# Two hybrid decoder layers on one core: the next mixer's first products on unnormalised h in both halves, six weight blocks split ahead and kept in DRAM, and another order of GpSimd memsets

## The chip, the core and the metric

The kernel runs on one core of a Trainium2 chip. The core has a matrix engine (TensorE, PE in the profile; its weight loads are PEld), VectorE (DVE), ScalarE (ACT), GpSimd (POOL) and a queue engine (SyncE, SP) that here issues nearly all DMAs. Each engine works through its own queue in order, and engines wait for one another by semaphores. The metric is the device time of one execution in microseconds; lower is better.

## What is computed

The reference is two layers of a trunk with 528 tokens (16 learned meta tokens and 512 real ones) and width 1024. Cut to what matters here:

```python
def rms_norm(x, g):
    return x * rsqrt(mean(x * x, -1) + 1e-6) * g

def mixer_sublayer(h, pre_g, post_g, w_in, ...):
    u = rms_norm(h, pre_g)
    z = u @ w_in
    q, k, v, f_logit, a_val, a_gate, sc_b, sc_c, sc_x = split(z)
    y_attn = forgetting_attention(q, k, v, log_sigmoid(f_logit + b_forget))
    a = a_val * sigmoid(a_gate)
    y_conv = silu(layer_norm(causal_depthwise_conv(a, 31 taps))) @ a_pw_w
    y_sc = sc_b * causal_depthwise_conv(sc_c * sc_x, 3 taps)
    y = head_rms_norm(concat[y_attn, y_conv, y_sc]) @ w_out
    return h + rms_norm(y, post_g)

def ffn_sublayer(h, pre_g, post_g, w_up, conv_w, w_down):
    z = causal_depthwise_conv(rms_norm(h, pre_g) @ w_up, 3 taps)
    g, up = split(z)
    return h + rms_norm((silu(g) * up) @ w_down, post_g)

for l in range(2):
    h = mixer_sublayer(h, ...); h = ffn_sublayer(h, ...)
```

The factor of a norm is one number per token. So w_in can be applied to h times the gain before the factor is known, and the product multiplied by the factor afterwards; a gate or a convolution needs the factor before its own non-linear step.

## The kernel before

Everything lies transposed: 128 partitions hold channels, the free axis holds the 528 tokens. h is a tile of eight k-blocks of 128 channels. Tokens are worked on in two halves of 264. Each float32 operand is split into a high part (a copy rounded to the matmul's format) and the rest, hi and lo, and each product is three matmuls, hi·hi, hi·lo and lo·hi, in `mm3` (L656). Weights come from DRAM in blocks of 128 output columns, 128 x 1024 for a full one: SP loads `raw` (3 buffers), ACT casts it to `whi`, DVE subtracts to `wlo`. The tiles `whi`/`wlo` come from a pool of three (`wp`) or, for some blocks, from a second pool of five on the other side of the memory (`wide_pool`, `wx`). Within the plain FFN loops this is `prep_one` (L506 to L509), two blocks ahead; elsewhere it is `plan_block` (L618 to L626).

The order of the engines' queues is written at build time by a planner, `Flow`. Work for ACT, DVE, POOL and SP is entered with an estimated duration, what it waits for, and a priority (a smaller number goes first); matmuls come from generators ("threads"), of which the earliest listed one that is ready goes on. The planner follows time with its estimates and fixes one order per engine. What it doesn't know, such as the reuse of memory by a later tile or the order of GpSimd's memsets, is waited for on the chip.

The place of the change is the step from layer 0's FFN to layer 1's mixer.

- `finish` (L1728) computes the last third of the FFN's down projection. `products` issues, for output blocks 0 and 1, both halves, then blocks 2 to 7 for half 0, then blocks 2 to 7 for half 1. `evac` (L1692) adds each result to `yp`, squares it on ACT (L744) and scales it by the post gain (L1695).
- `post_norm` forms the norm factor of y for a half. `Norms.factor` sums the squares by a matmul with a constant matrix (L793) and then needs three steps on ACT (L803, L806, L807) and two on DVE (L808, L814). Then yp is multiplied by it (L870) and added to h (L880), by pairs of k-blocks. h is squared again for the next norm, and goes to DRAM (`h_dram`) for a later use.
- `gained` (L823) writes h times layer 1's gain into yp, two ACT steps for each pair. `pre_norm` forms h's factor, multiplies yp by it on DVE (L835), casts to `uhi` on ACT (L837) and subtracts to `ulo` on DVE (L838).
- `first_half` issues layer 1's first six products for half 0: a_gate 0, a_val 0, a_gate 1, a_val 1, then sc_c 0 and sc_x 0. `First.steps` takes blocks 0 and 1 together, then blocks 2 to 5 together, going through k with all blocks of the group.
- `mixer` takes half 1 of the same six blocks (`firsts`): 0 and 1, then 2 and 3 when the gate of half 0 that holds their banks is done, then 4 and 5. `Front.gated` (L925 to L939) turns gate and value into the input `apad` of the 31-tap convolution: exp, log and exp on ACT, and a product on DVE. It can also take the norm factor, and does so for layer 0's half 0, where the factor is multiplied in twice on DVE. The 31 taps on two tiles (L969, L972) are low in priority on DVE. `sc_c` and `sc_x` evacuate blocks 4 and 5.
- After that, the pool `ap` of the attention opens, POOL clears its tiles (L418 and L1191 among them), and `fill` works through v, q, k and the rest by `mixer_steps`. v's first product also gives the forget gate's logits: DVE adds the bias into `fx` (L1217), and a chain from there (L1248 to L1262) has two small matmuls (L1261 the second).

Memory around it: `fp` holds the FFN's tiles, yp, rz (the factor), four tiles z, h, squares. The next mixer's tiles take the place of fp's; ap's take that of the five wide weight slots.

Of the kernel before, what the change touches and what calls it, by code (L numbers as in the profile page):

```python
# [9 lines left out]
F32 = mybir.dt.float32  # L10
# [5 lines left out]
P = 128  # L16
# [56 lines left out]
def chunk_list():  # L73
# [3 lines left out]
    for l in range(DEPTH):  # L77
# [5 lines left out]
        for kind, j in mixer_steps():  # L83
# [45 lines left out]
def mixer_steps():  # L129


    return [("sc_c", 0), ("sc_x", 0), ("v", 0), ("q", 0), ("k", 0), ("sc_b", 0), ("q", 1),
            ("k", 1), ("q", 2), ("k", 2), ("v", 1), ("q", 3), ("pw", 0), ("k", 3), ("sc_c", 1), ("sc_x", 1), ("sc_b", 1)]
# [56 lines left out]
class When:  # L190
# [170 lines left out]
def tile_hybrid_trunk(ctx: ExitStack, tc: tile.TileContext, xT, wflat, pv_d, out):  # L361
# [149 lines left out]

    def prefetch(n):
# [71 lines left out]
    coming = deque()  # L584

# [23 lines left out]
    def plan_block(i, prio):  # L609
# [18 lines left out]

        got = flow.op("sp", dma_us(sz), load, prio=prio, lat=dma_lat(sz), takes=[(raws, slot)])
        ring = split["pw"][chunks[i][1]] if chunks[i][0] == "a_pw_w" else split["wide" if i in wide else "rot"]  # L630
# [3 lines left out]
        a = act(act_us(sz), high, got, *after, prio=prio, takes=[(ring, b.slot)])  # L634
# [33 lines left out]
    class First:  # L668
# [9 lines left out]
        def alone(self, hf, both, *ids):  # L678
# [3 lines left out]
            for j, i in enumerate(ids):  # L682
                self.ps[hf, i] = t[:, j, :self.n[hf]] if both else t[:, :self.n[hf]]
                yield [self.ws[i].tok]
                for k in range(KD):
                    yield [When(lambda: self.at.get((hf, k)))]
# [139 lines left out]
    def pre_norm(norms, key, hg, hg_at, a, z, at, hf, prio):  # L826

        n = z - a
        yield from norms.factor(key, n)
        s = norms.sums[key]  # L830

        def pair(k, prio):
            y = hg[:, k:k + 2, a:z]
            hi = uhi[:, k:k + 2, a:z]
            f = dve(dve_us(2 * n), lambda: nc.vector.tensor_mul(y, y, s["r"].unsqueeze(1).to_broadcast([P, 2, n])),  # L835
                    s["r_at"], *hg_at[hf, k], prio=prio)
            c = act(act_us(2 * n), lambda: nc.scalar.copy(hi, y), f, prio=prio)  # L837
            d = dve(dve_us(2 * n), lambda: nc.vector.tensor_sub(ulo[:, k:k + 2, a:z], y, hi.bitcast(F32)), c, prio=prio)  # L838
            at[hf, k] = [c, d]
            return f  # L840

        s["free"].close(*[pair(k, prio + 0.01 * k) for k in range(0, KD, 2)])

    def post_norm(norms, key, nkey, h, h_at, a, z, yp, g, g_next, at, hf, prio, out_at, y_out, on_pe=()):
# [99 lines left out]
    def mixer(l, ypool, first, close_first, spans, front=None, rz0=None):  # L944
# [1143 lines left out]
```

## Time and profile before

| | |
|---|---|
| median of 3 runs | 1301.95 us (1300.68 to 1302.2) |
| the profiled execution | 1301.88 us, span 1300.2 us |
| mean granted TensorE clock | 0.997 |
| busy: PE, DVE, ACT, POOL | 1278.3, 852.7, 612.2, 96.2 us |
| weight loads by SP | 160 of 512 KB, 32 of 448 KB, 4 of 528 KB, 2 of 256 KB |

A row of a timeline has start, duration (of all instructions that it merges), engine, line, operation, output<-input, shapes, count, and in brackets the idle time before it with what ended it. A row of the waits has who waited for whom, the total in us, how often, and the longest. A row of windows has, for each engine, busy time and in brackets the count of instructions. Matmuls overlap in the records: the time between two starts is what one costs, not its duration.

The layers stand in the span like this: layer 0's mixer to about 222 us, its FFN to about 651 us, layer 1's mixer to about 870 us, then layer 1's FFN. The down projections of FFN parts 0 and 1 of layer 0 begin near 360 and 488 us.

### The profile page before, as it was taken

How to read it: one execution, taken by the hardware profiler on the slowest of the kernel's cores; microseconds unless marked ns; L12 is line 12 of the kernel's file. 1: busy time of each engine (PE TensorE's matmuls, PEld its weight loads, DVE VectorE, ACT ScalarE, POOL GpSimd, SP SyncE). 2: the span in 40 equal slices, each digit the busy share in tenths (PEclk: the TensorE clock that was granted, in tenths of full speed). 3: DMA queues.
4: the chain of work that ended last, by engine and by line, in shares of the span. 5: the costliest groups of instructions: out<-in, count | busy, mean ns of one | idle time of the engine just before them, and what ended most of it. 6: DMA issues, size and time to landing. Idle time of an engine off the chain costs nothing. (4 is left out here: it accounts for less than half of the span.)

```text
span 1300.2 us, 23941 instructions
## 1 busy us (share of the span) xinstructions
PE 1278.3 (98%) x9802; PEld 1226.7 (94%) x9802; DVE 852.7 (66%) x1449; ACT 612.2 (47%) x1143; POOL 96.2 (7%) x254
## 2 busy tenths in 40 slices
PE   8999999999999999999989999999999999999997
PEld 8999899999999999999989998899999799989997
DVE  7798765687624663566676877757786256636664
ACT  7254577654423432344662645866543234314443
POOL 1313311000000000000003133100000000000000
PEclk9999999999999999999989999999999999999999
DMA  6136132502232222223340361334032332232321
GB/s 238 34 100 158 50 99 78 201 18 98 82 98 83 96 79 101 95 83 100 105 142 18 108 166 43 97 125 147 18 103 92 97 88 89 72 122 86 92 72 65
DMA packets 46637, 124.75 MB, mean 96 GB/s; under 512 B 5616, under 2 KB 15984, under 8 KB 46528
## 3 DMA queue, kind: packets, MB, share of 16 engines
q1 hardware_dynamic: 46480, 123.10, 30.7%
q8 instruction: 77, 1.26, 0.4%
q14 instruction: 32, 0.26, 0.1%
q0 software_dynamic: 48, 0.13, 0.0%
HBM read 108.04 MB, written 4.33 MB: 86 GB/s over the span
## 5 line engine op out<-in xcount | busy, mean ns | idle before, releaser
L656 PE MATMUL psum<-uhi,whi 128*128 128x264 f32 (+1 forms) x1936 | 454.9, 287 | 2.8 <-ACT uhi L837 1.1
L656 PE MATMUL psum<-ulo,whi 128*128 128x264 f32 (+1 forms) x1936 | 449.2, 285 | 0.8 <-DVE ulo L1869 0.4
L656 PE MATMUL psum<-uhi,wlo 128*128 128x264 f32 (+1 forms) x1936 | 447.3, 284 | 0.0
L656 PEld LDWEIGHTS psum<-uhi,whi 128*128 128x128 f32 x1936 | 324.0, 189 | 8.2 <-issue 1.9
L656 PEld LDWEIGHTS psum<-ulo,whi 128*128 128x128 f32 x1936 | 325.0, 189 | 1.9 <-DVE ulo L1869 0.6
L656 PEld LDWEIGHTS psum<-uhi,wlo 128*128 128x128 f32 x1936 | 324.8, 189 | 0.0
L656 PE MATMUL psum<-yhi,whi 128*128 128x264 f32 (+3 forms) x888 | 247.7, 302 | 1.4 <-ACT yp L2020 1.0
L656 PE MATMUL psum<-yhi,wlo 128*128 128x264 f32 (+3 forms) x888 | 245.4, 299 | 0.7 <-DVE wlo L626 0.7
L656 PE MATMUL psum<-ylo,whi 128*128 128x264 f32 (+3 forms) x888 | 245.0, 298 | 0.0
L508 ACT CAST whi<-raw 128x1024 fp32r<-128x1024 f32 (+1 forms) x110 | 113.3, 1031 | 214.7 <-PE psum L656 200.3
L509 DVE TENSOR_TENSOR wlo<-raw,whi 128x1024 fp32r<-128x1024 f32 (+1 forms) x110 | 132.0, 1200 | 81.7 <-ACT whi L508 79.7
L656 PEld LDWEIGHTS psum<-yhi,whi 128*128 128x128 f32 x888 | 159.0, 188 | 8.7 <-ACT yp L2020 1.4
L656 PEld LDWEIGHTS psum<-yhi,wlo 128*128 128x128 f32 x888 | 159.1, 188 | 6.4 <-DVE wlo L626 1.1
L656 PEld LDWEIGHTS psum<-ylo,whi 128*128 128x128 f32 x888 | 159.3, 188 | 5.4
L1969 DVE SCALAR_TENSOR_TENSOR c<-z,pv,c 128x528 f32<-128x528 f32 (+1 forms) x176 | 131.9, 756 | 2.7
L626 DVE TENSOR_TENSOR wlo<-raw,whi 128x1024 fp32r<-128x1024 f32 (+2 forms) x86 | 102.5, 1204 | 33.6 <-ACT whi L622 30.9
L622 ACT CAST whi<-raw 128x1024 fp32r<-128x1024 f32 (+2 forms) x86 | 87.9, 1030 | 31.1 <-PE psum L656 19.7
L972 DVE SCALAR_TENSOR_TENSOR cacc<-apad,pv,cacc 128x528 f32<-128x528 f32 x120 | 87.6, 771 | 0.2
L1987 ACT CAST yhi<-c 128x528 fp32r<-128x528 f32 (+1 forms) x44 | 27.6, 627 | 108.6 <-DVE c L1983 108.6
L1979 ACT ACTIVATE c<-c 128x528 f32<-128x528 f32 (+1 forms) x44 | 28.1, 639 | 79.3 <-DVE c L1969 79.3
L1967 ACT ACTIVATE c<-z,pv 128x528 f32<-128x528 f32 (+1 forms) x88 | 63.3, 726 | 0.4 <-DVE z L1935 0.4
L1932 DVE TENSOR_TENSOR z<-psum,rz 128x528 f32<-128x528 f32 x40 | 28.3, 708 | 53.7 <-PE psum L656 52.2
(214 smaller groups left out, 1417.2 us busy)
## 6 DMA issues: line engine op xcount, KB each, us to landing
raw<-in_w_dram SPq DMA_DIRECT2D x160, 512.0 KB, 3.6
raw<-in_w_dram SPq DMA_DIRECT2D x32, 448.0 KB, 3.5
h<-in_x_dram SPq DMA_DIRECT2D x16, 264.0 KB
q<-pair_hi SPq DMA_DIRECT2D x24, 132.0 KB, 2.2
k<-pair_hi SPq DMA_DIRECT2D x24, 132.0 KB, 2.4
raw<-in_w_dram SPq DMA_DIRECT2D x4, 528.0 KB, 3.4
h_dram<-h SPq DMA_DIRECT2D x4, 528.0 KB
h<-h_dram SPq DMA_DIRECT2D x8, 264.0 KB, 5.8
```

Of the source, the lines that this page charges most:

```text
L508: nc.scalar.copy(hi[:, :sz], raw[:, :sz])
L509: nc.vector.tensor_sub(lo[:, :sz], raw[:, :sz], hi[:, :sz].bitcast(F32))
L622: nc.scalar.copy(box["hi"][:, :sz], box["raw"][:, :sz])
L626: nc.vector.tensor_sub(lo[:, :sz], box["raw"][:, :sz], box["hi"][:, :sz].bitcast(F32))
L656: nc.tensor.matmul(d, lhsT=w[a][:, k, cols], rhs=rhs(b, k, hf), start=start and i == 0 and p == 0, stop=stop and i == n - 1 and p == 2)
L972: nc.vector.scalar_tensor_tensor(conv[j], in0=src, in1=conv[j], scalar=col("a_dw_w", CK * j + i), op0=ALU.mult, op1=ALU.add)
L1932: nc.vector.tensor_mul(two(t[:, off:]), srcs[0], two(rz))
L1967: nc.scalar.activation(dst, src[:, 2:2 + 2 * fw], AF.Copy, scale=wtap(2, t))
L1969: nc.vector.scalar_tensor_tensor(dst, in0=src[:, i:i + 2 * fw], scalar=wtap(i, t), in1=dst, op0=ALU.mult, op1=ALU.add)
L1979: silu = nc.scalar.activation(cs[0], cs[0], AF.Silu)
L1987: nc.scalar.copy(ghi, cs[0])
```

## The change

**First products.** In the step between the layers, `post_norm` now writes h times the next gain, unnormalised, split into hi and lo, for both halves (`to=raw[hf]`): two scaled copies on ACT and two scalar_tensor_tensor on DVE for each pair, right behind L880. The tiles are the seven of the FFN's gated product, the down projection's right-hand side, and one more. `First` reads them. h's factor goes into `rz` for both halves and the normalised uhi and ulo follow with priorities 2.4 to 2.6, where they had 0 to 1.1. In the mixer the gates of both halves, and `sc_c`, get the factor (`rzs`): two DVE multiplications more for each gate, and two in place of an ACT copy for `sc_c`. yp and rz move to a pool `hg` on the wide slots' side, which closes with them; the second scratch of the norms is z0. `first_half` takes blocks 2 and 3, then 4, then 5 one after the other. The mixer's run goes on until u is planned.

**Weights.** `MASK` picks layer 1's first six w_in blocks. In layer 0's FFN, after every second output block of the down projections of parts 0 and 1, `store_one` splits one that was fetched the time before, writes hi and lo to DRAM from GpSimd's queue, and fetches the next raw block. Later `plan_block` loads hi and lo of these six straight into their weight tiles by two DMAs on SP, with no cast or subtraction.

**Memsets.** fx, gt and p4 of the mixer are made and cleared directly after vals, ahead of causal, k, q and dm, in both layers.

`mixer_steps` now looks up one list per layer; both lists are the old one.

```diff
+MASK = "111111000000000000000000"
...
+class Ahead:
+    def __init__(self, tok, by):
+        self.tok, self.by = tok, by
+    @property
+    def time(self):
+        return None if self.tok.time is None else self.tok.time - self.by
...
+    to_store = deque(i for i, c in enumerate(chunks) if c[1] == 1 and c[0] == "w_in" and MASK[sum(d[:2] == c[:2] for d in chunks[:i])] == "1")
+    stored = {}
+    fetched = deque()
+    def store_one():
+        if fetched:
+            i, sz, raw = fetched.popleft()
+            hi, lo = (T(wx[0], [P, WCHUNK], F32R, t) if sz <= WCHUNK else T(wp, [P, CHUNK], F32R, t) for t in ("whi", "wlo"))
+            nc.scalar.copy(hi[:, :sz], raw[:, :sz])
+            nc.vector.tensor_sub(lo[:, :sz], raw[:, :sz], hi[:, :sz].bitcast(F32))
+            stored[i] = T(dram, [P, 2, sz], F32, f"w_split{i}")
+            for n, t in enumerate((hi, lo)):
+                nc.gpsimd.dma_start(stored[i][:, n], t[:, :sz].bitcast(F32))
+        if to_store:
+            i = to_store.popleft()
+            sz = chunks[i][3] * chunk_cols(chunks[i])
+            raw = T(wp, [P, CHUNK], F32, "raw", 3)
+            nc.sync.dma_start(raw[:, :sz], wflat[offs[i]:offs[i] + P * sz].rearrange("(p s) -> p s", p=P))
+            fetched.append((i, sz, raw))
...
+        if i in stored:
+            def fetch(n):
+                if n == 0:
+                    box["w"] = [wtile(i, t) for t in ("whi", "wlo")]
+                    b.w = tuple(t[:, :sz].rearrange("p (k n) -> p k n", n=n_cols) for t in box["w"])
+                nc.sync.dma_start(box["w"][n][:, :sz].bitcast(F32), stored[i][:, n])
+            n_cols, lat = n, dma_lat(sz)
+            got = flow.op("sp", dma_us(sz), lambda: fetch(0), taken.get(id(ring), ()), prio=prio, lat=lat, takes=[(ring, b.slot)])
+            taken[id(ring)] = issued = [Ahead(got, lat)]
+            b.tok = flow.op("sp", dma_us(sz), lambda: fetch(1), issued, prio=prio, lat=lat)
+            coming.append((i, b))
+            return
...
@@ post_norm
-                    hi, lo, gc = uhi[:, k + i, a:z], ulo[:, k + i, a:z], g_next[:, k + i:k + i + 1]
+                    hi, lo = (uhi[:, k + i, a:z], ulo[:, k + i, a:z]) if to is None else (to[0][k + i], to[1][k + i])
+                    gc = g_next[:, k + i:k + i + 1]
...
@@ mixer
-                gated(1, j, first.tok[1, 2 * j + 1])
+                gated(1, j, first.tok[1, 2 * j + 1], rzs[1], zero)
...
-                gated(0, j, first.tok[0, 2 * j + 1])
+                gated(0, j, first.tok[0, 2 * j + 1], rzs[0], zero)
...
-                evacs += use(hf, first.ps[hf, i], first.tok[hf, 5], rz0 if hf == 0 else None)
-        flow.run(lambda: all(t.time is not None for t in evacs + list(gated_at.values())))
+                evacs += use(hf, first.ps[hf, i], first.tok[hf, 5], rzs[hf])
+        flow.run(lambda: all(t.time is not None for t in sum(u_at.values(), evacs + list(gated_at.values()))))
...
         mset(vals[:, :, :, DH:], 1.0)
+        fx = T(ap, [P, 5, HEADS], F32, "fx")
+        nc.gpsimd.memset(fx, 0.0)
+        gt = T(ap, [P, 5, HEADS], F32, "gt")
+        p4 = [T(ap, [P, N_META], F32, f"p4{i}") for i in range(2)]
+        for t in p4:
+            mset(t, 0.0)
...
@@ finish
-                hg_at = {(hf, k): gained(h, yp, a, z, k, gpre, out_at[hf, k], hf + 0.05 + 0.01 * k) for k in range(0, KD, 2)}
-                yield from pre_norm(norms, ("h", hf), yp, hg_at, a, z, first.at, hf, hf)
+                late = rzs[hf] is not None
+                hg_at = {(hf, k): gained(h, yp, a, z, k, gpre, out_at[hf, k], (2.4 if late else 0.05) + hf * (0.1 if late else 1) + 0.01 * k)
+                         for k in range(0, KD, 2)}
+                yield from pre_norm(norms, hf, n[hf], yp, hg_at, rzs[hf], u_at if late else first.at, 2.5 + 0.1 * hf if late else hf)
...
@@ first_half
-            yield from first.steps(0, (True, 2, 3), (False, 4), (False, 5))
+            yield from first.alone(0, True, 2, 3)
+            for i in (4, 5):
+                yield from first.alone(0, False, i)
...
-            yp = T(fp, [P, KD, L], F32, "yp", 1)
+            hp = wxs.enter_context(tc.tile_pool(name=f"hg{l}", bufs=1, side="right", reuse_waits="tile"))
+            rz, yp = T(hp, [P, L], F32, "rz"), T(hp, [P, KD, L], F32, "yp")
...
+                        if l == 0 and m%2:
+                            store_one()
...
+                    if not final:
+                        raw = [[g[f0 + k][b] for k in range(nf)] + [T(ypool, [P, L], F32R, f"y{n}{nf}")] for b, n in enumerate(("hi", "lo"))]
+                        raw = [[[t[:, half_sl(hf)] for t in ts] for ts in raw] if hf < 2 else None for hf in range(2)]
+                        rzs = [rz[:, half_sl(hf)] if raw[hf] else None for hf in range(2)]
+                        first = First(lambda b, k, hf, raw=raw: raw[hf][b][k] if raw[hf] else u_rhs(b, k, hf), [H, H], {})
...
-                        norms.factors([rs, rz], h=APART)
+                        norms.factors([rs, zs[0][:, 2:]], h=APART)
```

More of the change, by code (lines that the diff above doesn't have):

```diff
@@ L633, in plan_block @@
             after, prio = [coming[-1][1].tok], URGENT
-        a = act(act_us(sz), high, got, *after, prio=prio, takes=[(ring, b.slot)])
+        a = act(act_us(sz), high, got, *after, *(taken.get(id(ring), ()) if stored else ()), prio=prio, takes=[(ring, b.slot)])
+        taken[id(ring)] = [a]
         b.tok = dve(dve_us(sz), low, a, prio=prio)
@@ L1189, in mixer @@
             dms.append(dm)
-        fx = T(ap, [P, 5, HEADS], F32, "fx")
-        nc.gpsimd.memset(fx, 0.0)
-        gt = T(ap, [P, 5, HEADS], F32, "gt")
         g_hl = [T(mp, [P, L], F32, "sq", 2)[:HEADS].bitcast(F32R) for _ in range(2)]
-        p4 = [T(ap, [P, N_META], F32, f"p4{i}") for i in range(2)]
-        for t in p4:
-            mset(t, 0.0)
         v_at = {}
@@ L1776, in ends @@
             yield from post_norm(norms, ("y", hf), None if first is None else ("h", hf), h, [] if merge else list(h_at.values()), a, z, yp,
-                                 gpost if merge and not GA else None, None if merge else gpre, first and first.at, hf, hf, out_at, y_out, (0, 2) if alone and hf else ())
+                                 gpost if merge and not GA else None, None if raw and raw[hf] is None else gpre, first and first.at,
+                                 hf, hf, out_at, y_out, (0, 2) if alone and hf else (), raw and raw[hf])
             if first is None:
```

58 lines of the change are left out of this document (30 added, 28 removed), and 3 rows, old and new, of the table ORDERS.

## Prediction

> **What bounds the kernel now.** I read the page first, then the stages by windows, then TensorE's timeline where its share drops, then the two engines that feed it.
>
> ```profile
> span 1300.2 us, 23941 instructions
> PE 1278.3 (98%) x9802; PEld 1226.7 (94%) x9802; DVE 852.7 (66%) x1449; ACT 612.2 (47%) x1143; POOL 96.2 (7%) x254
> ```
>
> TensorE sets the end: 98% busy, with 21.9 us idle in all. A change that leaves the products alone can only win from those 21.9 us and from stretches at a reduced clock. The stage of the change is 605 to 720 us; columns below are busy time and count of PE, PEld, DVE, ACT, POOL, then granted clock, DMA share, GB/s.
>
> ```profile
> 640.00:650.00 10.00, 10.00 (x74) 9.61 (x73) 9.71 (x14) 8.81 (x18) 0.00 (x0) 1.00 0.41 128
> 650.00:660.00 10.00, 6.53 (x31) 5.28 (x30) 8.54 (x16) 9.24 (x19) 0.00 (x0) 0.71 0.41 141
> 660.00:670.00 10.00, 10.00 (x79) 10.00 (x79) 9.63 (x13) 6.89 (x14) 0.00 (x0) 0.95 0.67 220
> 670.00:680.00 10.00, 10.00 (x75) 9.61 (x74) 5.25 (x9) 3.30 (x7) 0.00 (x0) 1.00 0.31 101
> 680.00:690.00 10.00, 10.00 (x85) 10.00 (x84) 4.49 (x8) 5.01 (x11) 0.18 (x2) 1.00 0.17 55
> 710.00:720.00 10.00, 9.20 (x77) 8.83 (x76) 9.78 (x23) 5.32 (x11) 0.00 (x0) 1.00 0.29 75
> ```
>
> One row stands out: 31 matmuls in 650 to 660, where neighbours have 74 and 79, and a granted clock of 0.71. TensorE's timeline there:
>
> ```profile
> 648.39 1.05 PE L793 MATMUL psum<-c,om_d 128*128 128x264 f32 x4
> 649.09 0.48 PE L656 MATMUL psum<-yhi,whi 128*128 128x264 f32 x1
> 649.41 0.29 PE L656 MATMUL psum<-ylo,whi 128*128 128x264 f32 x1
> ...
> 650.87 0.28 PE L656 MATMUL psum<-ylo,whi 128*128 128x264 f32 x1
> 650.99 0.28 PE L656 MATMUL psum<-yhi,wlo 128*128 128x264 f32 x1
> 653.49 1.42 PE L793 MATMUL psum<-acc,om_d 128*128 128x264 f32 x4 [2.22 <-DVE acc L753]
> 656.01 0.59 PE L656 MATMUL psum<-uhi,whi 128*128 128x264 f32 x1 [1.09 <-ACT uhi L837]
> 656.75 0.59 PE L656 MATMUL psum<-ulo,whi 128*128 128x264 f32 x1 [0.15 <-DVE ulo L838]
> ...
> 660.88 0.38 PE L656 MATMUL psum<-ulo,whi 128*128 128x264 f32 x1
> 661.09 0.29 PE L656 MATMUL psum<-uhi,wlo 128*128 128x264 f32 x1
> ```
>
> The last product of layer 0's FFN issues at 650.99, the first of layer 1 at 656.01, because the normalised input of half 0 is not there. Then the matmuls are slow until 661.09: 20 of them from 656.01 on, where the spacing before the gap was 0.12 us (650.87 to 650.99).
>
> What half 0 waits for is a chain on ACT and DVE:
>
> ```profile
> 639.42 0.70 DVE L880 TENSOR_TENSOR h<-h,yp 128x528 f32<-128x528 f32 x1
> 645.98 0.70 DVE L880 TENSOR_TENSOR h<-h,yp 128x528 f32<-128x528 f32 x1
> 646.60 3.49 DVE L626 TENSOR_TENSOR wlo<-raw,whi 128x1024 fp32r<-128x1024 f32 x3
> 652.39 0.43 DVE L814 SCALAR_TENSOR_TENSOR rz<-rz 128x264 f32<-128x264 f32 x1
> 655.99 1.55 DVE L838 TENSOR_TENSOR ulo<-yp,uhi 128x528 fp32r<-128x528 f32 x2
> ```
>
> The new h of half 0 is there pair by pair from 640.1 to 646.7 (L880), but its norm factor only at 652.8 (L814), and scaling and splitting (L835, L837, L838) follow.
>
> **Part 1, first products on unnormalised h.** The factor leaves the path. Now each pair of k needs, behind L880, two scaled copies on ACT and two subtractions on DVE; the factor multiplies the products later, in the evacuations. Nearest rows for these two and for the next steps of half 1:
>
> ```profile
> L823 ACT ACTIVATE yp<-h,pg x16: 500/502/505, 640.7 to 669.6; 128x264 f32<-128x264 f32 x16
> 658.41 0.42 DVE L814 SCALAR_TENSOR_TENSOR rs<-rs 128x264 f32<-128x264 f32 x1
> 659.38 2.35 DVE L626 TENSOR_TENSOR wlo<-raw,whi 128x1024 fp32r<-128x1024 f32 x2
> 661.65 1.32 DVE L870 TENSOR_TENSOR yp<-yp,rs 128x528 f32<-128x528 f32 x2
> 680.73 0.71 DVE L838 TENSOR_TENSOR ulo<-yp,uhi 128x528 fp32r<-128x528 f32 x1 [0.70 <-ACT uhi L837]
> 683.65 0.42 DVE L939 TENSOR_TENSOR apad<-psum,cxp 128x264 f32<-128x264 f32 x1
> ```
>
> Half 0: 8 copies of 0.50 (4.0 us ACT) and 8 subtractions of 0.42 (3.4 us DVE) between 640 and 650. DVE drops the 3.49 us of weight splits at 646.60 there (part 2), so it breaks even; the last pair should be split at about 649.5 (645.98 + 0.70 + 3.4 at the most 650.1), and the product loop reaches it only after three earlier pairs. I take no wait at 651. TensorE then runs: 650.99 + 0.12, the four norm matmuls of half 1's y (648.39 to 649.41 holds four of them and one product, so 1.02 - 0.12 = 0.90 us), and 20 matmuls of 0.122: the twenty-first at 651.11 + 0.90 + 2.44 = 654.45 instead of 661.09. **Gain 6.6 us**: the gap and the half clock together.
>
> Half 0's six blocks are 144 matmuls, 17.5 us, and the twelve norm matmuls of h (0.225 each, 2.7 us) fall among them: TensorE wants half 1 at 651.1 + 0.9 + 17.5 + 2.7 = 672.2. Half 1's y factor is done at 658.8 (L814) at the latest; then 4 multiplications, 4 additions (0.66 each by L870's 1.32 for two) and 8 subtractions of 0.42 are 8.6 us of DVE: 667.4, without the 2.35 us of splits that stood ahead of them. Cover 4.8 us. If it were gone, every microsecond shows.
>
> Behind that, the gates (L925 to L939) of half 0 must clear banks before blocks 2 and 3 of half 1 can start, at 672.2 + 5.9 = 678.1. Today they sit behind ulo (680.73) and end at 684.07. They get two DVE multiplications by the factor each (0.42 x 4 = 1.7 us): their present 683.65 + 0.42 - 681.44 = 2.6 us become some 4.3 us from 672.2, 676.5. Cover 1.6 us, thin. The eight gates' multiplications and four of sc_c (replacing two ACT copies) add 12 x 0.42 = 5.0 us of DVE.
>
> Normalised u is still made, for v, q and k, now last in priority: over both halves 16 copies on ACT, 8 multiplications, 8 casts and 8 subtractions, as before. v starts at 672.2 + 17.5 = 689.7. DVE has 9.7 us of work in 670 to 690 today, so 10 us are free for what is left of it. I cost it at nothing; what hides it are half 1's 17.5 us of products.
>
> **Part 2, six blocks split in the FFN.** Six loads on SP's queue, six casts on ACT and six subtractions on DVE move to the down projections of FFN parts 0 and 1; twelve stores of 512 KB are new on POOL's queue; between the layers twelve loads of 512 KB on SP replace six.
>
> ```profile
> 389.47 1.05 ACT L508 CAST whi<-raw 128x1024 fp32r<-128x1024 f32 x1 [4.31 <-PE psum L656]
> 390.55 1.22 DVE L509 TENSOR_TENSOR wlo<-raw,whi 128x1024 fp32r<-128x1024 f32 x1 [4.63 <-ACT whi L508]
> 395.33 1.05 ACT L508 CAST whi<-raw 128x1024 fp32r<-128x1024 f32 x1 [4.32 <-PE psum L656]
> raw<-in_w_dram SPq DMA_DIRECT2D x160, 512.0 KB, 3.6
> ```
>
> In the FFN a block lasts 395.33 - 389.47 = 5.86 us and ACT and DVE idle 4.3 and 4.6 of them; 1.05 and 1.22 more at every second block fit. A raw buffer is held between two such steps, so the stream runs on two of three for that long: a load may then start when the block two earlier is split, 5.9 us (1.05 + 1.22 + 3.6) before it lands, and it has two blocks, 11.7 us. POOL does nothing in the FFN; the stores have 100 us before they are read. Cost 0; bounds 0 and six exposed splits, 6 x 2.27 = 13.6 us.
>
> Between the layers the loads wait for a weight slot, freed by the last product on it, and SP's queue behind them holds h's stores and v's loads. The last slot frees at 651.1; two loads, estimated at twice 3.6 us, land by 658.3, and block 5 is wanted at 652.0 + 14.6 = 666.6. Nothing.
>
> **Part 3, memset order.**
>
> ```profile
> DVE fx L1217 <- POOL p L418: 12.2, 2, 6.3
> 692.46 1.04 POOL L418 MEMSET vals<- 128x528 f32 x2
> 704.91 0.14 POOL L1191 MEMSET fx<- 128x40 f32 x1
> PE psum L1261 <- DVE fpre L1256: 1.7, 2, 0.9
> ```
>
> In both mixers DVE's queue stands for about 6 us behind fx, whose clearing needs 0.14 us but comes on POOL's queue 12.4 us after vals, behind the memsets for k, q and dm. Clearing it right after vals, near 693.5 in today's times, takes away that stall. DVE has slack at its end, so most of the 12.2 us are worth nothing; what TensorE loses later is the wait for fpre, 1.7 us in two places, when DVE has caught up too late. fx's last addition would come some 2 us earlier, more than 0.9. **Gain 1.7 us**, bounds 0 and 1.7.
>
> **Sum.** 1301.88 (the profiled execution; span 1300.2 and 1.68 around it; the median of the runs, 1301.95, is 0.07 above) - 6.6 - 1.7 = 1293.6. For the thin cover at the gates and for small misses of an order fixed beforehand I add 0.5, between 0 and 3.3 (today's two idle times at this place, 2.22 + 1.09): **1294.1 us**.
>
> **Rivals.** *B: part of the gap stays.* TensorE runs in order; if half 1's norm matmuls are put ahead of the first products, as today, they again wait for acc, 2.22 us, and 1.09 us may follow for the last splits. Against it: half 0's splits are ready by then, so the products can be put first. Price 3.3 us, 1297.4; with the slow matmuls again (20 x 0.10 = 2.0), 1299.4. Here the granted clock fell to half after a 2.22 us gap, four matmuls and a 1.09 us gap, so I count the 2.0. The Trainium skill (TensorE: Matmul & The Clock Gate, Part 1) says the clock halves after an idle window of about 3.4 us; by that, a single gap of 2.2 us would cost only itself, 1296.3, and the trace agrees with it only if its two gaps count as one.
>
> *C: the wait moves to the gates or to half 1.* Cover 1.6 and 4.8 us; a late u op or two ahead of a gate (0.7 each) and scratch shared with the norms speak for it. Taken at 2 us: 1296.1.
>
> *D: slower, through the FFN's weight stream.* If the held buffer keeps a block's split behind TensorE's need, the six steps are exposed: 13.6 us, 1294.1 + 13.6 = 1307.7. It decides once a load needs over 11.7 - 2.3 = 9.4 us to land where the row has 3.6, so I give it little.
>
> *E: hidden anyway.* From 705 us DVE is the busy engine (9.78 of 10 in 710 to 720) and feeds attention. If it, not TensorE, paces that stage, the 6.6 us come back as waits there and only part 3 remains: 1301.9 - 1.7 = 1300.2. For it: 5.0 us more DVE work. Against: its 6.3 us stall behind fx falls away in the same stretch, and TensorE is 92% busy even there.
>
> **Chances.** A, the forecast, 0.55 (its own range 1292.4 to 1295.6); B 0.16; C 0.12; E 0.09; D 0.08. This measurement cannot tell under 0.2%, 2.6 us, from no change: faster is below 1299.3, slower above 1304.6. Faster: A, C and nearly all of B, 0.82. Same: E and B's edge, 0.10. Slower: D, 0.08. The range reaches from 1291.5 (A with 2 us of further relief on DVE in attention) to 1299.4 (B's dear end), leaving out D, E and little below.
>
> **What would show it.** Right: no TensorE idle over 1 us between the last down product and the first with the new input, granted clock 1.00 throughout there; v starting about 6.6 us earlier; fx's wait on POOL and fpre's wait gone in both layers; FFN parts 0 and 1 of layer 0 as long as before. Wrong: a wait for hi, lo or a loaded block at 651 or near 672, for a gate near 678, gaps at the FFN's blocks, or the gain shrinking between v and the output projection.

## The result, and the profile after

The changed kernel takes 1294.19 us (median of 4 runs, 1293.85 to 1294.39); the kernel before, run beside it, 1301.84 us (4 runs, 1300.68 to 1302.2). The ratio is 0.9942, 95% interval 0.993 to 0.9954: faster by 7.65 us. 1294.1 was predicted. The profiled execution has a span of 1292.0 us, 8.2 less than the 1300.2 of before.

The head of the page:

```profile
span 1292.0 us, 24062 instructions
PE 1274.1 (99%) x9802; PEld 1223.7 (95%) x9802; DVE 864.3 (67%) x1477; ACT 618.1 (48%) x1157; POOL 103.1 (8%) x266
```

TensorE does the same 9802 matmuls. Its idle time falls from 21.9 to 17.9 us and its busy time by 4.2 us; slow matmuls at the half clock count as busy (before, 660 to 661 us: 6 matmuls at clock 0.50, busy 1.00). VectorE has 11.6 us more work and ScalarE 5.9 us, and the kernel is faster all the same. The stage of the change, by windows, with the columns of the table before:

```profile
640.00:650.00 10.00, 10.00 (x78) 9.74 (x77) 8.87 (x17) 8.84 (x20) 0.00 (x0) 1.00 0.96 337
650.00:660.00 10.00, 10.00 (x78) 9.74 (x77) 6.99 (x15) 7.91 (x20) 0.00 (x0) 1.00 0.74 282
660.00:670.00 10.00, 10.00 (x75) 9.61 (x74) 8.69 (x16) 7.29 (x17) 0.00 (x0) 1.00 0.31 108
670.00:680.00 10.00, 9.31 (x76) 9.10 (x76) 8.73 (x18) 8.03 (x18) 0.18 (x2) 1.00 0.01 2
```

In 650 to 660 stand 78 matmuls at a granted clock of 1.00, where 31 stood at 0.71. TensorE's timeline at the old gap:

```profile
651.07 0.28 PE L712 MATMUL psum<-ylo,whi 128*128 128x264 f32 x1
651.19 0.28 PE L712 MATMUL psum<-yhi,wlo 128*128 128x264 f32 x1
651.32 1.05 PE L849 MATMUL psum<-acc,om_d 128*128 128x264 f32 x4
652.20 1.05 PE L849 MATMUL psum<-c,om_d 128*128 128x264 f32 x4
652.90 0.48 PE L712 MATMUL psum<-yhi,whi 128*128 128x264 f32 x1
```

The norm matmuls on acc, for which TensorE had waited 2.22 us, now issue without a wait. Both traces have 8520 products in `mm3`; the 4441st, the first of layer 1, stood at 656.01 behind the gap, and is now at 648.24, 0.12 us behind the one before it: eighteen products on the unnormalised pairs (the last two of them above) go ahead of the norm. A new, small wait shows 20 us later, in the row of TensorE's timeline at the start of half 1:

```profile
672.27 0.39 PE L712 MATMUL psum<-yhi,whi 128*128 128x264 f32 x1 [0.69 <-DVE z L864]
```

To see where the time went, the n-th matmul of one trace is set against the n-th of the other: the table gives its start before and the shift after. A step between two rows is time won or lost between these two matmuls. (In 5150 to 5250 the order of the norm matmuls among the products differs, so single rows there mean little.)

| matmul | place | start before, us | shift after, us |
|---|---|---|---|
| 450 | layer 0's mixer, ahead of the wait for fpre | 63.24 | -0.67 |
| 560 | behind it | 78.06 | -1.78 |
| 2770 | layer 0's FFN, near the start of part 0's down projection | 365.72 | -1.98 |
| 2790 | behind it | 368.16 | -1.73 |
| 3840 | behind the start of part 1's down projection | 496.33 | -1.11 |
| 5250 | layer 1's first products, end of half 0 | 678.52 | -7.84 |
| 5260 | start of half 1 | 679.73 | -6.86 |
| 5400 | v, just behind its start | 696.79 | -6.82 |
| 5600 | behind layer 1's wait for fpre | 722.65 | -8.03 |
| 9800 | end | 1294.38 | -8.49 |

So: the gap and the half clock -6.7 us; part 3 -1.1 and -1.2 around the waits for fpre; the FFN of layer 0 +0.25 and +0.6; the start of half 1 +1.0. Part 3 has one more step ahead of the first row: at matmul 412 the kernel before loses 0.21 us, because a weight load of layer 0's v waits for fx, and the kernel after does not. The other -0.46 of the opening hold nothing of the change: they differ from execution to execution (the variants below with the same opening stand 0.2 to 0.7 us behind the kernel after at matmul 450). Two small rests were not followed: -0.2 between matmuls 560 and 2770, and the last -0.45, most of it one step in layer 1's FFN.

The two costs have their rows. First the FFN: VectorE's first and last row of the last gate of part 1 in the kernel before; then, in the kernel after, ScalarE's and VectorE's timelines at the same gate, and TensorE's row behind them.

```profile
483.51 0.71 DVE L1932 TENSOR_TENSOR z<-psum,rz 128x528 f32<-128x528 f32 x1 [2.51 <-PE psum L656]
488.31 0.71 DVE L1988 TENSOR_TENSOR ylo<-c,yhi 128x528 fp32r<-128x528 f32 x1 [0.70 <-ACT yhi L1987]
```

```profile
481.00 1.05 ACT L541 CAST whi<-raw 128x1024 fp32r<-128x1024 f32 x1 [1.06 <-DMA raw<-in_w_dram]
481.78 0.71 DVE L1992 TENSOR_TENSOR z<-psum,rz 128x528 f32<-128x528 f32 x1 [2.51 <-PE psum L712]
482.41 1.22 DVE L542 TENSOR_TENSOR wlo<-raw,whi 128x1024 fp32r<-128x1024 f32 x1
483.54 1.08 DVE L528 TENSOR_TENSOR wlo<-raw,whi 128x896 fp32r<-128x896 f32 x1
484.54 1.57 DVE L2029 SCALAR_TENSOR_TENSOR c<-z,pv,c 128x528 f32<-128x528 f32 x2
487.56 0.71 DVE L2048 TENSOR_TENSOR ylo<-c,yhi 128x528 fp32r<-128x528 f32 x1 [0.70 <-ACT yhi L2047]
492.31 0.51 PE L712 MATMUL psum<-yhi,whi 128*128 128x264 f32 x2 [0.31 <-DVE yp L2082]
```

The split of a block for layer 1 (L541, L542) stands inside the last gate of part 1, between the factor's product (L1992) and the convolution (L2029). From L1992 to the gate's last row, L2048, 487.56 - 481.78 = 5.78 us pass; before it was 488.31 - 483.51 = 4.80. The program places the step behind the down projection's second, fourth, ... block, but its raw data are there early and the engines' order, made at build time, has it some 20 us ahead of that. The last gate of part 0 has a split inside as well (L541 at 352.25) and is 0.97 us longer. Of these two delays TensorE loses 0.6 and 0.25 us.

Then half 1's start: ScalarE's timeline at its three steps of the norm factor of half 1's h (L859, L862, L863).

```profile
669.41 0.48 ACT L859 ACTIVATE z<-psum,c_rms 128x264 f32<-128x264 f32 x1 [2.37 <-PE psum L849]
669.79 0.50 ACT L879 ACTIVATE yp<-h,pg 128x264 f32<-128x264 f32 x1
670.20 0.41 ACT L862 ACTIVATE z<-z 128x264 f32<-128x264 f32 x1
670.51 0.62 ACT L892 CAST uhi<-yp 128x528 fp32r<-128x528 f32 x1
671.03 0.43 ACT L863 ACTIVATE z<-z 128x264 f32<-128x264 f32 x1
```

Between the three steps stand two of the late operations for the normalised u (L879, L892), and VectorE puts one of 0.71 us (L893, at 671.16) ahead of the factor's next step, L864 at 671.79, which reads the norm's sum out of its bank. TensorE's 0.69 us wait ends on it.

Last, GpSimd and VectorE behind the opening of the pool ap:

```profile
690.71 0.78 POOL L437 MEMSET vals<- 128x528 f32 x2 [4.09 <-DVE sccx L1068]
691.41 0.13 POOL L1217 MEMSET fx<- 128x40 f32 x1
693.20 0.17 DVE L1271 TENSOR_TENSOR fx<-psum,pv 128x8 f32<-128x8 f32 x1 [0.92 <-ACT vals L1267]
```

fx is clear at 691.5 us and VectorE no longer stands behind it. But GpSimd's clearing as a whole begins *later* against v than it did: vals at 690.71 with v at 689.97, where it was 692.46 with v at 696.79. What releases it is named in the row: the evacuation of sc_c (L1068), the last reader of rz in the program, whose new place closes just before ap opens. This turned out to matter (experiment 2).

### The profile page after: what moved, and what is told of

It is laid out like the page before. It is cut to its first block, busy times and chain, and to the rows that moved or that the text cites. A ratio compares the mean times of both kernels' runs of the same rounds, so it can differ in the third digit from the quotient of the medians.

```text
span 1292.0 us, 24062 instructions
## 1 busy us (share of the span) xinstructions
PE 1274.1 (99%) x9802; PEld 1223.7 (95%) x9802; DVE 864.3 (67%) x1477; ACT 618.1 (48%) x1157; POOL 103.1 (8%) x266
## 5 line engine op out<-in xcount | busy, mean ns | idle before, releaser
L712 PE MATMUL psum<-uhi,whi 128*128 128x264 f32 (+1 forms) x1840 | 426.0, 287 | 1.6 <-ACT uhi L1927 0.8
L712 PE MATMUL psum<-ulo,whi 128*128 128x264 f32 (+1 forms) x1840 | 420.8, 284 | 0.6 <-DVE ulo L1929 0.4
L712 PE MATMUL psum<-uhi,wlo 128*128 128x264 f32 (+1 forms) x1840 | 418.8, 283 | 0.0
L712 PEld LDWEIGHTS psum<-uhi,whi 128*128 128x128 f32 x1840 | 304.9, 188 | 6.1 <-issue 1.6
L712 PEld LDWEIGHTS psum<-ulo,whi 128*128 128x128 f32 x1840 | 305.9, 189 | 1.4 <-DVE ulo L1929 0.6
L712 PEld LDWEIGHTS psum<-uhi,wlo 128*128 128x128 f32 x1840 | 305.6, 189 | 0.0
L712 PE MATMUL psum<-yhi,whi 128*128 128x264 f32 (+3 forms) x984 | 275.8, 301 | 2.4 <-ACT yp L2080 1.0
L712 PE MATMUL psum<-yhi,wlo 128*128 128x264 f32 (+3 forms) x984 | 272.9, 297 | 1.1 <-DVE wlo L668 1.1
L712 PE MATMUL psum<-ylo,whi 128*128 128x264 f32 (+3 forms) x984 | 272.3, 297 | 0.0
L712 PEld LDWEIGHTS psum<-yhi,wlo 128*128 128x128 f32 x984 | 177.3, 188 | 6.8 <-DVE wlo L668 1.5
L2029 DVE SCALAR_TENSOR_TENSOR c<-z,pv,c 128x528 f32<-128x528 f32 (+1 forms) x176 | 131.9, 756 | 2.7
L664 ACT CAST whi<-raw 128x1024 fp32r<-128x1024 f32 (+2 forms) x80 | 81.8, 1030 | 25.6 <-PE psum L712 17.9
L1992 DVE TENSOR_TENSOR z<-psum,rz 128x528 f32<-128x528 f32 x40 | 28.3, 708 | 53.7 <-PE psum L712 52.2
```

The lines of the kernel that those rows point to most:

```text
L664: nc.scalar.copy(box["hi"][:, :sz], box["raw"][:, :sz])
L712: nc.tensor.matmul(d, lhsT=w[a][:, k, cols], rhs=rhs(b, k, hf), start=start and i == 0 and p == 0, stop=stop and i == n - 1 and p == 2)
L1992: nc.vector.tensor_mul(two(t[:, off:]), srcs[0], two(rz))
L2029: nc.vector.scalar_tensor_tensor(dst, in0=src[:, i:i + 2 * fw], scalar=wtap(i, t), in1=dst, op0=ALU.mult, op1=ALU.add)
```

## The experiments

Every kernel ran beside the kernel before (medians of 1301.76 to 1301.78 us). Shifts are again those of n-th matmuls. The intervals of many pairs of experiments overlap; differences of a few tenths of a microsecond rest on the place of a shift in the traces, not on the times.

| | kernel | median, us | ratio to before, 95% interval |
|---|---|---|---|
| 1 | before, with part 3 alone | 1299.37 | 0.9981 (0.9972 to 0.9991) |
| 2 | after, with the old memset order | 1301.27 | 0.9998 (0.9988 to 1.0007) |
| 3 | after, no block split ahead | 1299.56 | 0.9983 (0.9973 to 0.9992) |
| 4 | after, unnormalised h in neither half | 1298.04 | 0.9969 (0.9958 to 0.998) |
| 5 | after, unnormalised h in half 0 only | 1295.04 | 0.9949 (0.9936 to 0.9963) |
| 6 | after, late u operations give way | 1293.33 | 0.9935 (0.9922 to 0.9949) |
| 7 | after, all splits in FFN part 0 | 1294.57 | 0.9945 (0.9933 to 0.9958) |
| 8 | after, only fx cleared early | 1294.41 | 0.9946 (0.9933 to 0.996) |
| 9 | 5 and 6 together | 1293.99 | 0.9942 (0.9929 to 0.9956) |
| 10 | 6, three blocks split ahead | 1294.52 | 0.9947 (0.9933 to 0.996) |
| 11 | 6, splits two blocks later | 1292.94 | 0.9934 (0.992 to 0.9947) |

**1. Part 3 alone.** The kernel before, with fx, gt and p4 made and cleared behind vals, as in the change's last hunk.

> The kernel before with part 3 alone: fx, gt and p4 cleared right after vals. My theory, from matching the n-th matmul of both profiles: each mixer gives 1.2 to 1.3 us, so 1301.84 - 2.5 = 1299.3 us. Rival, the prediction's sum: only the wait for fpre, 1.7 us in all, 1300.1. Second rival: alone, layer 1 gives nothing since its queue still stands behind the unchanged step between the layers, 1300.6. In the trace the waits of fx for POOL and of the L1261 matmul for fpre are gone in all three.

Measured 1299.37, 2.4 us under the kernel before beside it. The shift goes from -0.27 to -1.36 at layer 0's wait for fpre and from -1.37 to -2.59 in layer 1, and 0.21 us are won at matmul 412: 2.5 us, as in the kernel after.

**2. The whole change without part 3.**

```diff
         mset(vals[:, :, :, DH:], 1.0)
-        fx = T(ap, [P, 5, HEADS], F32, "fx")
-        nc.gpsimd.memset(fx, 0.0)
-        gt = T(ap, [P, 5, HEADS], F32, "gt")
-        p4 = ...
...
             dms.append(dm)
+        fx = T(ap, [P, 5, HEADS], F32, "fx")
+        nc.gpsimd.memset(fx, 0.0)
+        gt = T(ap, [P, 5, HEADS], F32, "gt")
+        p4 = ...
```

> The changed kernel with the old memset order. If the parts add up: 1294.19 + 2.5 = 1296.7 us. Rival: in layer 1 the stall behind fx is hidden by the earlier start of the taps, and only layer 0 loses its 1.3: 1295.5.

Both missed. It takes 1301.27: parts 1 and 2 alone win nothing. Layer 0 loses the expected 1.3 us, and at v, matmul 5400, the kernel is still 1.70 us behind the kernel after; at matmul 5500 it is 7.01 behind. The wait on TensorE, then the rows of GpSimd, VectorE and TensorE:

```profile
PE psum L1284 <- DVE fx L1273: 3.5, 1, 3.5
```

```profile
692.40 0.77 POOL L437 MEMSET vals<- 128x528 f32 x2 [4.08 <-DVE sccx L1068]
703.38 0.14 POOL L1247 MEMSET fx<- 128x40 f32 x1
703.55 0.17 DVE L1273 TENSOR_TENSOR fx<-psum,pv 128x8 f32<-128x8 f32 x1 [9.73 <-POOL p L437]
699.95 0.28 PE L1284 MATMUL psum<-wlo,uhi 128*128 128x264 f32 x1
703.77 0.39 PE L1284 MATMUL psum<-whi,uhi 128*128 128x264 f32 x1 [3.54 <-DVE fx L1273]
```

v's products need a free bank; a bank of v is free when fx's addition has read the logits out of it (L1273), and that addition waits for the clearing of fx at the end of GpSimd's list. v starts at 691.66 in this trace, so fx is cleared at v + 11.7. Before, it was v + 8.1 (704.91 - 696.79), and fx's addition ended at v + 8.46. In this trace the last product ahead of the wait starts at 699.95 and one product takes 0.12 us, so TensorE wants the bank at 700.07, v + 8.4. The old order was thus at the edge already: in the kernel before, a weight load of v waits 0.16 us for fx's addition at 705.30, and 0.2 us are lost there (matmul 5470). Part 1 brings v 6.8 us forward but GpSimd's list only 1.75 us (692.46 to 690.71 in the kernel after), and the whole list of 11 us is then too late. The list's late start is what does it: without the 4.08 us that GpSimd waits for L1068, fx would be clear at 699.30, v + 7.6 (an estimate from these rows; no run leaves rz at its old place). Behind the wait the clock falls as well:

```profile
700.00:710.00 10.00, 6.46 (x41) 5.88 (x41) 6.42 (x12) 0.75 (x2) 3.34 (x11) 0.83 0.00 0
```

**8. Only fx.** The kernel after, with gt and p4 back at the old place and fx alone cleared behind vals.

> The kernel after, with only fx cleared behind vals; gt and p4 are made and cleared at the old place, behind k, q and dm. Theory: in the kernel after with the whole old order, v's banks waited 3.5 us for fx's addition on VectorE, and that one for the clearing of fx at 703.4 us; nothing else of the order matters. Then this is the kernel after: 1293.8 to 1294.6 us, no wait for fx on TensorE. Rival: p4 or gt is waited for as well, or the later memsets go on holding VectorE: 1295.5 to 1301.3 us, with a wait for p4 or gt in its place.

Measured 1294.41. Behind the opening, at the end of which it stands 0.43 us behind the kernel after, the shift to it stays between 0.33 and 0.61 us to the end. One clearing of 0.13 us, moved ahead in one queue, is all of part 3.

**3. No block split ahead.** `MASK` all zeros; the six blocks are loaded and split between the layers.

> The changed kernel with no block stored (the mask all zeros): the six loads, casts and subtractions are back between the layers, and the FFN is as before. My theory: they are what makes room on DVE and ACT for the new splits of h; three subtractions (3.5 us) and three casts (3.1 us) come back into 638 to 650, TensorE waits some 3 us at 651 or for blocks 4 and 5, perhaps with slow matmuls behind it, and the FFN gives back 0.9: 1296 to 1299 us. Rival: the room was there without it, and part 2 costs only its 0.9: 1293.3.

Measured 1299.56, 0.56 above the theory's band, and the place was wrong: no wait at 651 us. The gap is gone without part 2 as well (against the kernel before the shift goes from -1.62 at matmul 3840 to -8.24 at 5150). The FFN gets its 0.85 us back; then TensorE waits where the kernel after has its 0.69:

```profile
PE psum L712 <- DVE z L864: 2.3, 1, 2.3
670.00:680.00 10.00, 7.66 (x59) 7.18 (x59) 7.91 (x18) 6.96 (x15) 0.18 (x2) 1.00 0.22 75
```

At v it is 1.2 us behind the kernel after; the other 3.8 us come behind it, most of them in layer 1's attention (+4.5 at matmul 6800). TensorE's waits name a part of these: 1.0 us for pair_lo (L1420) and 0.9 us in two for ylo (L1186), neither of which stands in the kernel after. Why they come later stays open, and so with it what most of part 2 is worth. The profiled execution took 1298.40, 1.2 us under the median, so its trace does not show the whole price.

**4. Unnormalised h in neither half.** Splits and memset order stay; the condition `hf < 2`, which picks the halves, becomes `hf < 0`.

> The changed kernel with unnormalised products in neither half: parts 2 and 3 alone. My theory: half 0 still waits for the norm factor, which hangs on squares and matmuls, so the gap of about 5 us and the half clock stay; part 3 gives 2.5, part 2 costs 0.9 in the FFN and frees up to 1.5 us in the chain: 1298.5 to 1300.2. Rival: the six splits were the delay in the chain, and most of the gain is there without unnormalised products: 1295 to 1296.

Measured 1298.04, half a microsecond under the expected band. Taking the six splits out of the stage wins 2 us at the old gap (the shift to before goes from -0.83 at matmul 5070 to -2.85 at 5150), and the wait for the norm stays; the two ends of the gap have become one:

```profile
PE psum L849 <- DVE acc L809: 3.4, 2, 2.8
650.00:660.00 10.00, 7.19 (x43) 6.57 (x42) 8.73 (x16) 5.40 (x11) 0.00 (x0) 0.83 0.79 302
```

So of the 6.7 us at the gap part 2 alone brings 2.0, and part 1 on top of it 4.7. The split depends on the order: part 1 without part 2 brings 6.6 there (experiment 3).

**5. Unnormalised h in half 0 only.** The same condition as `hf < 1`.

> The changed kernel with unnormalised products in half 0 only; half 1 takes the normalised input as before. My theory: the gap at 651 is gone, but half 1's input is late in its place: TensorE wants it near 671.5, its factor comes near 672.7, and product, cast and subtraction of the first pair bring it to some 675; 3 to 4 us of waiting, and slow matmuls if the clock falls (up to 2 us more): 1297 to 1300 us. Rival: half 1 has cover enough and its part of the change is worth nothing: 1294.2.

My theory fell: 1295.04. Behind the stage (matmul 5600) the kernel is 0.14 us behind the kernel after, less than the 0.25 from the opening: half 1's unnormalised product wins nothing there. TensorE's wait near 672 us is about as long as in the kernel after, for the normalised ulo of half 1 in place of the factor:

```profile
PE psum L712 <- DVE ulo L893: 0.6, 1, 0.6
```

The other 0.5 us are lost between matmuls 5600 and 7000.

**6. Late operations give way.** `YE = 2` for 9: in this stretch the planner then holds back an operation of priority 2 or later (those for the late u of half 0 are) when an earlier one will be ready soon.

> The changed kernel with the planner's rule for yielding switched on in this stage: an op of priority 2 or more gives way when one of better priority will be ready within 0.6 of its duration. My theory: in the changed kernel TensorE waits 0.69 us at 671.6 for the bank that half 1's norm factor holds, because late copies, casts and subtractions of u stand between the steps of that factor on ACT and DVE; with the rule they stand back, and up to 0.9 us are won: 1293.3 to 1293.8. Rival: the wait is the chain's own length and stays, 1294.2, or the order gets worse elsewhere, above 1294.5.

Measured 1293.33. The late operations leave the factor's three steps alone (669.17, 669.69, 670.15 on ScalarE), the wait at 672 us is gone, and the shift to the kernel after goes from +0.47 to -0.50 there and stays to the end:

```profile
670.00:680.00 10.00, 10.00 (x84) 10.00 (x84) 8.84 (x18) 8.09 (x18) 0.18 (x2) 1.00 0.01 2
```

**9. Half 0 only, and late operations give way.**

> Unnormalised h in half 0 only, and the late u operations give way to earlier ones (YE = 2). Half 0 only cost 0.6 to 0.85 us against the kernel after, and giving way alone won 0.5 to 0.9. Theory: what half 1's unnormalised product still wins is only cover against the late operations of half 0, so with these giving way it wins nothing: 1293.1 to 1293.7 us, as with both halves and giving way (1293.33). Rival: half 1's factor, products and splits are themselves too late by 0.6 us or more: 1293.9 to 1294.4 us, with a wait for ulo or uhi of half 1 near 672 us.

The time, 1293.99, is in the rival's band and the mechanism is the theory's: against experiment 6 the shift is +0.25 at matmul 5070 and +0.27 at 5400, so the stage itself loses nothing, and no wait for ulo or uhi of half 1 is left. The rest is 0.30 us in the opening and 0.4 between matmuls 5600 and 7000, as in experiment 5; why half 1's edit wins that little in attention stays open.

**7. All splits in FFN part 0.**

```diff
-                        if l == 0 and m%2:
+                        if l == 0 and part == 0 and m:
                             store_one()
```

> The changed kernel with all seven store steps in part 0's down projection (after blocks 1 to 7) and none in part 1's. My theory: a split costs only where it lands in the last gate's chain just before a down projection, 0.25 us before part 0 and 0.6 before part 1; without part 1's the 0.6 are won: 1293.6. Rival: the cost follows the number of splits and the raw buffer they hold, and stays, 1294.2, or grows since every block then has one, up to 1295.

The rival. Part 1's 0.6 us come back, but the step at part 0's down projection grows from 0.25 us by another 0.96: a cast for layer 1 (363.00) now stands ahead of the copy that frees a bank.

```profile
363.00 1.05 ACT L541 CAST whi<-raw 128x1024 fp32r<-128x1024 f32 x1 [4.03 <-DMA raw<-in_w_dram]
363.96 1.04 ACT L527 CAST whi<-raw 128x1024 fp32r<-128x1024 f32 x1
364.90 0.59 ACT L2080 COPY yp<-psum 128x528 f32<-128x528 f32 x1
365.55 0.51 PE L712 MATMUL psum<-yhi,whi 128*128 128x264 f32 x2 [0.94 <-ACT yp L2080]
```

**11. The splits two output blocks later**, with the giving way of experiment 6.

```diff
-                        if l == 0 and m%2:
+                        if l == 0 and m in ((3, 5, 7), (3, 5, 6, 7))[part]:
                             store_one()
```

> Late u operations give way (YE = 2), and the steps that split and store stand after output blocks 3, 5, 7 of the down projection of FFN part 0 and 3, 5, 6, 7 of part 1, not 1, 3, 5, 7 of both. Theory: the splits cost time in the FFN only where they fall into the last gate's chain ahead of a down projection (352 us: 0.25 us, 482 us: 0.6 us); two blocks later none falls there, so 0.5 to 0.85 us of the 0.87 come back: 1292.4 to 1292.9 us. Rival: each step costs by itself wherever it stands, or they pile up in part 1: 1293.2 to 1294 us.

At the two places the theory holds, and all six splits now run inside the down projections: against experiment 6 the shift steps by -0.25 us at matmul 2780 and by -0.59 at 3820, and the last gate of part 1 takes 4.80 us again. Six splits elsewhere in the down projections cost nothing that shows. Of the 0.82 us won so far, 0.5 are given back in layer 1 (0.4 of it in one step near 934 us, where the kernel after had won 0.4 against the kernel before), so the time is 1292.94, 0.04 above the theory's band. It is the fastest median of all; the intervals of this and of experiment 6 overlap, so the 0.4 between them are not certain by the times.

**10. Three blocks split ahead.** `MASK = "000111..."`, with the giving way of 6.

> Only blocks 3 to 5 of layer 1's first six are split ahead and kept; blocks 0 to 2 are split between the layers, as in the kernel before; late u operations give way (YE = 2). Theory: blocks 0 to 2 add 3 x 1.05 us on ScalarE and 3 x 1.22 us on VectorE in the stretch in which half 0 is split, so its last splits come some 3.7 us later than 651.4 us and TensorE waits for one to two of them: 1295 to 1298 us, idle at 651 to 655 us. Rival: with no blocks kept, no wait stood at 651 us, only one of 2.3 us at 672 us that giving way takes off: 1293.0 to 1294.0 us, also because three splits less stand in layer 0's FFN.

1294.52, between the two. The mechanism is the theory's, at about half its price: TensorE waits for a weight split between the layers, and the kernel loses 1.5 us from matmul 5070 to 5150; 0.6 us come back in the FFN, where fewer steps stand, and 0.5 are lost behind matmul 5600.

```profile
650.66 0.39 PE L712 MATMUL psum<-yhi,wlo 128*128 128x264 f32 x1 [1.05 <-DVE wlo L668]
```

A variant with none of the six blocks kept and the late operations giving way, or with only the first two or three kept, was not tried.

## Why the prediction was right, step by step

**The gap and the half clock, predicted 6.6 us, measured 6.7.** All its parts held: no wait at 651 us, granted clock 1.00 throughout, v at 689.97 (predicted 689.7). One estimate under it was off without harm. The last pair of half 0 was to be split by 650.1 at the latest; VectorE's timeline shows 651.4:

```profile
649.06 0.70 DVE L935 TENSOR_TENSOR h<-h,yp 128x528 f32<-128x528 f32 x1
649.86 0.71 DVE L809 TENSOR_TENSOR acc<-acc,c 128x528 f32<-128x528 f32 x1
650.49 0.89 DVE L943 SCALAR_TENSOR_TENSOR ylo<-h,pg,yhi 128x264 fp32r<-128x264 f32 x2
```

The margin that the prediction named, that the product loop reaches the last pair after three earlier ones, covered the 1.3 us. Experiment 4 splits the step: without unnormalised h the wait for the norm stays, and 4.7 of the 6.7 us with it. What the prediction leaned on here and did not need is part 2: it let VectorE drop 3.49 us of weight splits at this place, but in experiment 3, with these splits back between the layers, the gap is gone too. Part 2's worth shows elsewhere, 2.0 us at the start of half 1 and 3.3 in attention, and the prediction priced neither as a gain of part 2.

**Part 3, predicted 1.7 us with bounds 0 and 1.7, measured 2.5: a right mechanism, mis-sized above its bound.** The 1.7 was the listed idle time in front of fpre (0.9 and 0.8). What a wait costs, though, is the distance between two starts. In layer 1 the listed idle is 0.80, and the distance between the matmul in front and the one that waited is 1.08, where the same two stand 0.10 apart in the kernel after: 0.98 us lost. The listed idle begins at the modelled end of the matmul before, 0.27 us after its start. Two such tails of 0.17, and 0.2 us in each layer at v's banks (matmuls 412 and 5470), where a weight load waited for fx, make up nearly all of the rest. The prediction had no term for these banks.

**Part 3 was also a condition of part 1, and the prediction missed that.** It summed the parts as if each stood alone and placed the clearing of fx "near 693.5 in today's times", 3.3 us ahead of v; it is now at v + 1.4. The step that failed, by the rows of experiment 2, is the move of yp and rz to the wide slots' side: the text on the change names it, but the prediction did not ask who reads rz last and what waits for the pool to close. Without part 3 the time is 1301.3, where the prediction's sum without its 1.7 gives 1295.8. That the case came out right all the same is luck in this: both parts happened to be in the change. Rival E had the shape of it (the gain comes back behind v), with VectorE as a pace maker; the runs show GpSimd's list.

**The FFN splits, predicted 0 (bounds 0 and 13.6), measured 0.85.** The step "1.05 and 1.22 more at every second block fit" was right for blocks inside a down projection, and experiment 11 shows that they cost nothing there. What failed is the place: the prediction took the steps where the program writes them, and two of six run ahead of the down projection, in the last gate's chain, where a delay of just under 1 us is more than TensorE's slack. Rival D's mechanism, a held buffer, shows in no row.

**Thin covers, predicted 0.5, measured 1.0.** It is rival C's kind, "a late u op or two ahead", at another place: in the factor of half 1's h, whose bank TensorE wants, rather than at a gate. Experiment 6 takes it off by order alone. The gates had their cover: half 0's last gate row ends at 677.27, 0.8 us past the estimate, and TensorE waited for no gate.

**The normalised u, predicted 0**, was not free: its operations are what made that 1.0. **Half 1's unnormalised product** was argued with its 4.8 us of cover; experiments 5 and 9 show that at this place it wins nothing, so the cover existed without it. The errors nearly cancel, which is luck too: 6.7 + 2.5 - 0.85 - 1.0 = 7.35 against 6.6 + 1.7 - 0.5 = 7.8.

**Rival B** (norm matmuls first) did not come. Its reading of the clock, a fall after both gaps of the kernel before, was wrong; the last section shows why.

## What to carry to other kernels

When a change brings a stage forward, list every engine's queue that does *not* come forward with it, and by how much each was on time before; here a memset of 0.13 us at the end of GpSimd's list was just at the edge, 0.2 us late, and took back all that parts 1 and 2 win. Work that "fits in an idle engine" has to be placed by where the engines run it, not by where the program writes it: inside the last gates' chains it cost 0.25 and 0.6 us, two blocks later nothing. And price a removed wait by the distance between starts rather than by the listed idle.

## What the runs showed of the hardware

The clock falls after a shorter idle time than I had counted on, and in fixed portions. Windows of 1 us, first before, then experiment 4, then experiment 3:

```profile
654.00:655.00 1.00, 0.92 (x3) 0.20 (x2) 1.00 (x3) 0.48 (x2) 0.00 (x0) 0.62 0.27 110
655.00:656.00 1.00, 0.00 (x0) 0.00 (x0) 0.93 (x3) 1.00 (x3) 0.00 (x0) 0.50 0.00 0
...
661.00:662.00 1.00, 1.00 (x10) 1.00 (x9) 1.00 (x2) 0.00 (x0) 0.00 (x0) 0.96 0.36 55
```

```profile
653.00:654.00 1.00, 0.76 (x2) 0.66 (x3) 1.00 (x3) 0.80 (x3) 0.00 (x0) 0.71 1.08 377
654.00:655.00 1.00, 1.00 (x4) 0.71 (x3) 1.00 (x3) 0.47 (x1) 0.00 (x0) 0.50 1.03 401
...
656.00:657.00 1.00, 1.00 (x7) 1.00 (x7) 0.28 (x1) 1.00 (x4) 0.00 (x0) 0.58 0.97 389
```

```profile
672.00:673.00 1.00, 0.00 (x0) 0.00 (x0) 0.03 (x1) 1.00 (x4) 0.00 (x0) 1.00 0.45 172
673.00:674.00 1.00, 0.54 (x4) 0.54 (x5) 1.00 (x3) 1.00 (x2) 0.00 (x0) 1.00 0.04 16
```

The length of a wait alone does not decide. In the kernel before the fall comes at 655 - 0.76 = 654.24, as the share 0.62 of its window gives it. That is behind the wait of 2.22 us and ahead of the one of 1.09 us (654.91 to 656.01), so the first alone halved the clock. A single wait of 2.34 us (experiment 3, 671.12 to 673.46) left it at 1.00; one of 2.81 us (experiment 4) halved it for 0.58 + 2 + 0.84 = 3.4 us. Before, where 1.09 us of idle time followed within the half clock, it lasted 0.76 + 6 + 0.08 = 6.8 us, two such portions.

The traces' own records of the clock, which are finer than these windows, fit one reading. The changes in a trace lie whole multiples of 3.4133 us apart, whatever TensorE does in between: before, full clock from 5.72, half from 654.25 (190 portions later), full from 661.08 (two more); in experiment 4 the same at 4.89, 653.42 (190) and 656.84 (one); in experiment 2 at 4.49, 704.22 (205) and 707.63 (one). The portion that ends with the fall held 2.22 us of waits before, 2.81 in experiment 4 and 2.96 of the 3.54 in experiment 2. In experiment 3 the record begins at 7.06, and an edge at 7.06 + 195 x 3.4133 = 672.65 cuts the wait into 1.53 and 0.81 us. So in these traces 2.2 us of idle time within one portion halved the clock for the next, and 1.5 us did not. Where between the two the limit lies, no run shows.

The Trainium skill (TensorE: Matmul & The Clock Gate, Part 1) speaks of a free-running activity window of about 3.4 us that decides on the clock. The portions agree with it in their length and in running on by themselves; an idle time of 2.22 us that is shorter than the window and still halves the clock does not agree with the rule that a whole idle window is needed, which the prediction had weighed in rival B.
